# Embedding products on the banks of scores and transposes, two first-stage blocks in the retrievals, six gathered rows in the second stage

## The chip, the cores and the metric

The kernel runs on one core of a Trainium2 chip. The metric is the device time of one execution in microseconds (us), the median of some runs. The engines are called as in the profile: PE (TensorE, matmuls), DVE (VectorE), ACT (ScalarE), POOL (GpSimd, which here only issues gathers), SP (SyncE, which issues the other transfers), and the 16 DMA engines. Every engine works through its own list of instructions in order. A tile framework builds these lists: a planner puts the instructions of the program in an order of its own, by priorities and its own costs, so that the order on an engine need not be the order in the source.

## The reference, cut to what matters

One layer of a decoder for 576 tokens (512 of a prompt, 64 of samples). Attention, a gating unit and their merge come first and are not touched. What matters here is the channel mixer, a retrieval over 16384 experts of one neuron each, and the embedding added after it:

```python
q = (xb @ w_q).reshape(blk, PEER_HEADS, 2, PEER_HALF)
sc = jnp.einsum('thcd,hcnd->thcn', q, sub_keys)
s_top, i_top = lax.top_k(sc, PEER_TOPK)
...
best, pos = lax.top_k(cand, PEER_TOPK)
idx = jnp.take_along_axis(cand_idx, pos, axis=-1)
gate = jax.nn.softmax(best, axis=-1)
act = jax.nn.gelu(jnp.einsum('thkd,td->thk', expert_u[idx], xb))
out = jnp.einsum('thk,thkd->td', gate * act, expert_v[idx])
...
x3 = x2 + sigmoid(rms_norm(x2) @ w_ple_gate) * (p @ w_ple)
```

## The kernel before

The tokens are split in two groups. For 192 of them (the samples and one prompt tile) the chosen rows of `peer_u` and `peer_v` are gathered, one row of 1024 numbers for each of 128 partitions at a time: POOL issues the gather (L726), and DVE multiplies the row and sums it up (L737 for `peer_u`, L744 for `peer_v`). There are 384 such gathered rows (192 of each table).

For the other 384 tokens the mixer is computed densely. A *first-stage block* (`stage1`, L781) multiplies 128 experts of `peer_u` with the 384 tokens: SP loads 512 KB of weights (L75), ACT and DVE split them into a high and a low part (`w_hi` L70, `w_lo` L71), PE runs 24 matmuls of 384 columns (L86), and ACT takes the gelu out of PSUM (L795). There are 128 such blocks. The *second stage* (L977) multiplies the gated result with `peer_v`, 18 matmuls for each of 128 turns (L1022). Blocks of the first stage and turns of the second alternate there until the former have run out.

In between, the gates are needed as a dense matrix. First come five *retrievals* (`retrieve`, L624), a long chain of small DVE instructions that finds for each token the indices and gates of its experts. `make_ew` (L801) transposes the result of one on PE. Then the *gate phase* runs 24 passes (`build_g`, L856; below "pass" 0 to 23), each for 16 tokens in four groups: DVE makes one-hots of the indices (`hot`, L870), ACT or DVE scales them (`og`, L876 or L879), PE multiplies them (eight matmuls, L887), ACT copies the product into the tile `gs` (L891), and at the end of a pass SP writes `gs` to DRAM (`gd`, L894, 1024 KB). `gs` has two buffers, which the passes use in turn. The last two retrievals are still running during the first seven passes.

PE fills its time in the retrievals and in the gate phase with first-stage blocks. Three tables say how many, and how many rows are gathered beside them. `S1_TOPK` is the number of blocks that are to be done by the end of the first, second and third retrieval; each block pays `GP[0]` = 0.5 of a gathered row once gathering has begun. In the gate phase a pass pays `GT[0]` rows for the first seven passes and `GT[1]` for the next fifteen, and the blocks are spread evenly from `S1_TOPK[2]` to 33 (`S1_PRE`) over the first seven passes and to 56 over the others. In the second stage a turn pays `G2[0]` for the first 44 turns, `G2[1]` as long as there are first-stage blocks, and `G2[2]` after that.

During the retrievals PE also computes the embedding products p @ w_ple (`ple`, L819): five tiles of tokens, each in two halves of six matmuls (L837), which ACT copies out (L839). Beside them `x1_rows` (L843) transposes rows of x1 for later (L851).

PSUM has eight banks here: two buffers each of "mm", "sc", "pv" and "pt". First-stage blocks take "mm" and "pv" by turns (L786). The group products of the gate phase take "sc" and "pt" by turns, the transposes of `x1_rows` and `make_ew` take "pt".

Of the kernel before, what the change touches and what calls it, by code (L numbers as in the profile page):

```python
# [25 lines left out]
TB = 16  # L26
JB = 8
GP = [0.5, 0.0, 1.65]
G2 = (1.45, 1.78, 2.06)
SPILL = set(range(2, 40, 2))  # L30
NSP = len(SPILL)
GT = (2.0, 2.9)
GS = 2.0 ** 14
TAIL0 = 112
TAIL1 = 122
S1_TOPK = (4, 9, 13)
TBK = 7
S1_END = 6
OPB = 4
# [12 lines left out]
def tile_decoder_step(ctx: ExitStack, tc: tile.TileContext, a, o):  # L52
# [16 lines left out]
    def split(src, hi, lo):  # L69
        A.activation(hi, src, AF.Copy)  # L70
        V.tensor_sub(lo, src, hi.bitcast(F32))  # L71
# [61 lines left out]
    def bank(tag):  # L133
        return psB.tile([P, 512], F32, name=tag)
# [47 lines left out]
    with tc.high_priority(offset=500):  # L182
        for cols in HALVES:
            ps = bank("sc")[:, :cols.stop - cols.start]
# [64 lines left out]
    for g in range(4):  # L249
# [7 lines left out]
        if g == 0:  # L257
            pv = bank("pt")
# [3 lines left out]
            pv = bank("pt")  # L262
# [279 lines left out]
    for c0, r in tilesA:  # L542
# [4 lines left out]
        for hh in range(2):  # L547
            hs = slice(hh * 512, (hh + 1) * 512)
            pt = bank("pt")
# [182 lines left out]
    def gather_steps():  # L732
        for ti, ns in ((0, NS), (1, P)):
            dots = gp.tile([P, P], F32, name="dots")
            for s in range(ns):
                row_ = gather_row(a["peer_u"], ixs[ti][:, s:s + 1])
                V.scalar_tensor_tensor(row_, row_, 1.0, xrs[ti], op0=ALU.mult, op1=ALU.mult,  # L737
                                       accum_out=dots[:, s:s + 1])
                yield
            A.activation(dots[:, :ns], dots[:, :ns], AF.Gelu_apprx_tanh)  # L740
            V.tensor_tensor(dots[:, :ns], dots[:, :ns], gts[ti][:, :ns], op=ALU.mult)
            for s in range(ns):
                row_ = gather_row(a["peer_v"], ixs[ti][:, s:s + 1])
                V.scalar_tensor_tensor(accs[ti], row_, dots[:, s:s + 1], accs[ti], op0=ALU.mult, op1=ALU.add)  # L744
                yield
# [23 lines left out]
    def pay(x):  # L769
        credit[0] += x  # L770
        n = int(credit[0])
        credit[0] -= n
        gather(n, mark_pe[0])
# [7 lines left out]
    def stage1():  # L781
        nonlocal j1, nlive
        j = j1
        j1 += 1
        w = load_block(a["peer_uT"][j])
        ps = (mm() if j % 2 or phase[0] > 1 else bank("pv"))[:, :NB]  # L786
        tform(ps, w, xb, first=g_last.get(len(g_last) - G_LAG))
        if j in SPILL:
            act = held_x[-1][:, sorted(SPILL).index(j) % 6, :]
        else:  # L790
            n = nlive % RING
            nlive += 1
            act = held_x[n // 6][:, n % 6, :] if n < NXP - 6 else (
                acp[0][:, n - NXP + 6, :] if n < RING - 6 else held_x[-1][:, n - RING + 6, :])
        A.activation(act, ps, AF.Gelu_apprx_tanh)  # L795
        acts[j] = act
        if j in SPILL:
            S.dma_start(ad[sorted(SPILL).index(j)], act)
        pay(GP[phase[0]])

    def make_ew(e0, e1_, gtf):  # L801
        pt = bank("pt")
        for q, src in enumerate((e0, e1_, gtf)):
            T.transpose(out=pt[:, q * P:(q + 1) * P], in_=src, identity=ident)
        ij = ep.tile([P, P // 2, 2, 2], F16, name="ij")
        gpk = ep.tile([P, P, 2], F16, name="gpk")
        for q in range(2):
            A.activation(ij[:, :, q, :], pt[:, q * P:(q + 1) * P].rearrange("p (u t) -> p u t", t=2), AF.Copy)
        V.tensor_scalar(gpk[:, :, 1], pt[:, 2 * P:3 * P], GS, 1.0 / GS, op0=ALU.mult, op1=ALU.max)
        V.scalar_tensor_tensor(gpk[:, :, 0], pt[:, 2 * P:3 * P], GS, gpk[:, :, 1], op0=ALU.mult, op1=ALU.subtract)  # L810
        ewT.append((ij, gpk))
# [7 lines left out]
    def ple():  # L819
        ws_ = []  # L820
        for k in range(2):
            raw = wp.tile([P, D], F32, name="w_raw", bufs=4)
            S.dma_start(raw, a["w_ple"][k])
            ws_.append([plp.tile([P, D], F32R, name=nm) for nm in ("wph", "wpl")])
            split(raw, *ws_[k])
        for c0, r in TILES:
            pt = plp.tile([P, 2, P], F32, name="pt")
            S.dma_start(pt[:, :, :r], a["pT"][:, :, c0:c0 + r])
            ph, pl = (plp.tile([P, 2, P], F32R, name=nm) for nm in ("ph", "pl"))
            split(pt[:, :, :r], ph[:, :, :r], pl[:, :, :r])  # L830
            for hh in range(2):
                st = plp.tile([P, 512], F32, name="st")
                ps = bank("pv")
                hs_ = slice(hh * 512, (hh + 1) * 512)
                for k in range(2):
                    for i, (xi, wi) in enumerate(((ph, 0), (ph, 1), (pl, 0))):
                        T.matmul(ps[:r], lhsT=xi[:, k, :r], rhs=ws_[k][wi][:, hs_],  # L837
                                 start=k == 0 and i == 0, stop=k == 1 and i == 2)
                A.activation(st[:r], ps[:r], AF.Copy)  # L839
                S.dma_start(pld[c0:c0 + r, hs_], st[:r])  # L840
            yield
# [14 lines left out]
    def build_g(tb):  # L856
# [37 lines left out]
        S.dma_start(gd[:, :, tb].rearrange("c p j t -> p c (j t)"), gs.rearrange("p (c j) t -> p c (j t)", j=JB))  # L894

    ples, xrs_ = ple(), x1_rows()
    for ti in range(3):
        for _ in retrieve(ti, ti < 2):
            if len(acts) < S1_TOPK[ti]:
                stage1()  # L900
# [3 lines left out]
        if ti == 0:  # L904
            steps.append(gather_steps())
        while len(acts) < S1_TOPK[ti]:
            stage1()
# [11 lines left out]
    for tb in range(NB // TB):  # L919
# [9 lines left out]
        if tb < TBK:  # L929
            goal = S1_TOPK[2] + (tb + 1) * (S1_PRE - S1_TOPK[2]) // TBK  # L930
        else:
# [6 lines left out]
        for _ in range(2):  # L938
            if rest_t and next(rest_t[0], 1) == 1:
                rest_t.pop(0)  # L940
                make_ew(*found[4 - len(rest_t)])
        pay(GT[tb >= TBK] if tb < 22 else 0)
    while nlive < RING - 1:
# [82 lines left out]
    for j in range(NJ):  # L1026
# [4 lines left out]
        if j and j - 1 not in SPILL and j1 < NJ:  # L1031
            stage1()
        pay(G2[0 if j < 44 else 1 if j1 < NJ else 2])
        if j == TAIL0:
# [185 lines left out]
```

## Time and profile before

| | |
|---|---|
| median of 3 runs | 1717.13 us (1714.81 to 1718.23) |
| the profiled execution | 1715.17 us |
| its span, first to last instruction | 1713.3 us |
| PE, share of the span | 98% |
| DVE | 82% |
| ACT | 47% |
| POOL | 31% |
| DMA, mean rate | 268 GB/s |

The retrievals with the embedding products run from about 497 to 572 us of the span, the gate phase from 575 to 816, with its eighth pass beginning at 661, and the second stage from 837 on. A busy share is a mean over stages with different limits. So the profile is read by stages: which engine is full there, and what each of PE's waits ended on.

### The profile page before, as it was taken

What the parts mean: (1) busy time and instruction counts of PE and PEld (TensorE: products, weight loads), DVE (VectorE), ACT (ScalarE), POOL (GpSimd) and SP (SyncE); (2) the same over time, 40 slices, a digit from 0 to 9 for tenths busy, and PEclk for the clock granted to TensorE, in tenths of its full rate; (3) what the DMA queues carried; (4) which work ended last, traced back from release to release, by engine and by line L of the source; (5) the groups of instructions that cost most, each with busy time, mean ns of one, the idle gap of its engine ahead of it and who ended that gap; (6) DMA issues with size and microseconds to landing.
All of it is one profiled execution on the core that took longest, in us unless ns stands there. A gap on an engine that the chain in (4) does not pass through costs nothing.

```text
span 1713.3 us, 27406 instructions
## 1 busy us (share of the span) xinstructions
PE 1680.2 (98%) x10040; PEld 1518.4 (89%) x10040; DVE 1406.5 (82%) x2725; ACT 806.9 (47%) x1399; POOL 536.2 (31%) x390
## 2 busy tenths in 40 slices
PE   8999999999999999899999999999999999999998
PEld 7988999999988899888988888899999888888877
DVE  7365566569899999898688899989888898999983
ACT  6566452343355888777433333333333433333352
POOL 0000000000002112343144454455565665666600
PEclk9999999999999999999999999999999999999999
DMA  6311222433247789999999999999999899999952
GB/s 235 101 54 59 75 96 87 156 111 103 72 160 262 238 265 303 347 393 359 326 341 367 366 379 396 397 395 369 374 356 365 329 380 344 356 378 375 375 198 80
DMA packets 179479, 459.11 MB, mean 268 GB/s; under 512 B 15504, under 2 KB 78992, under 8 KB 177296
## 3 DMA queue, kind: packets, MB, share of 16 engines
q1 hardware_dynamic: 123760, 255.29, 42.2%
q0 software_dynamic: 55584, 202.07, 31.6%
q8 instruction: 79, 1.29, 0.3%
q14 instruction: 56, 0.46, 0.1%
HBM read 420.67 MB, written 37.36 MB: 267 GB/s over the span
## 4 chain that ended last, share of the span: by engine, by line
PE 86%; DVE 6%; DMA 4%; ACT 3%; issue 1%; SPq 0%; ACTq 0%; DVEq 0%
PE mm L86 40%; PE oacc L1022 31%; PE pv L86 4%; DMA gd<-gs 3%; PE oacc L983 2%; DVE w_lo L71 1%; PE sc L86 1%; PE pt L887 1%; ACT w_hi L70 1%; PE mm L983 1%; PE sc L887 1%; PE sc L596 1%; PE pv L338 1%; ACT og L876 0%; DMA w_raw<-peer_uT 0%
## 5 line engine op out<-in xcount | busy, mean ns | idle before, releaser
L726 POOL DMA_INDIRECT row<-peer_u,idx x192 | 262.8, 1369 | 812.5 <-PE pv L86 470.3
L70 ACT ACTIVATE w_hi<-w_raw 128x1024 fp32r<-128x1024 f32 x321 | 340.0, 1059 | 372.2 <-PE mm L86 279.4
L71 DVE TENSOR_TENSOR w_lo<-w_raw,w_hi 128x1024 fp32r<-128x1024 f32 x321 | 391.4, 1219 | 80.9 <-ACT w_hi L70 79.8
L86 PE MATMUL mm<-xd,w_hi 128*128 128x384 f32 x1552 | 401.6, 337 | 0.0
L726 POOL DMA_INDIRECT row<-peer_v,idx x192 | 272.0, 1417 | 237.8 <-DVE acc L744 159.2
L86 PE MATMUL mm<-x,w_hi 128*128 128x320 f32 (+1 forms) x1504 | 308.1, 299 | 0.0
L86 PEld LDWEIGHTS mm<-xd,w_hi 128*128 128x128 f32 x1552 | 282.0, 188 | 6.5
L86 PE MATMUL mm<-xd,w_lo 128*128 128x384 f32 x776 | 262.0, 338 | 0.0
L744 DVE SCALAR_TENSOR_TENSOR acc<-row,dots,acc 128x1024 f32<-128x1024 f32 x192 | 245.4, 1278 | 4.8 <-DMA row<-peer_v,idx 4.6
L86 PEld LDWEIGHTS mm<-x,w_hi 128*128 128x128 f32 x1504 | 241.8, 190 | 8.2 <-issue 7.4
L737 DVE SCALAR_TENSOR_TENSOR row<-row,xr 128x1024 f32<-128x1024 f32 x192 | 232.1, 1219 | 14.0 <-DMA row<-peer_u,idx 14.0
L1022 PE MATMUL oacc<-w_hi,wh 128*128 128x512 f32 x768 | 241.2, 394 | 0.0
L1022 PE MATMUL oacc<-w_hi,wl 128*128 128x512 f32 x768 | 241.0, 394 | 0.0
L1022 PE MATMUL oacc<-w_lo,wh 128*128 128x512 f32 x768 | 240.9, 394 | 0.0
L86 PE MATMUL mm<-x,w_lo 128*128 128x320 f32 (+1 forms) x752 | 223.1, 297 | 0.0
L1022 PEld LDWEIGHTS oacc<-w_hi,wl 128*128 128x128 f32 x768 | 143.6, 187 | 35.5
L1022 PEld LDWEIGHTS oacc<-w_lo,wh 128*128 128x128 f32 x768 | 143.6, 187 | 35.5
L1022 PEld LDWEIGHTS oacc<-w_hi,wh 128*128 128x128 f32 x768 | 143.0, 187 | 29.4
L86 PEld LDWEIGHTS mm<-xd,w_lo 128*128 128x128 f32 x776 | 146.0, 188 | 0.0
L86 PEld LDWEIGHTS mm<-x,w_lo 128*128 128x128 f32 x752 | 142.4, 189 | 1.0 <-issue 0.8
L86 PE MATMUL pv<-xd,w_hi 128*128 128x384 f32 x496 | 133.8, 345 | 0.0
L70 ACT ACTIVATE wh<-x 128x384 fp32r<-128x384 f32 x66 | 34.6, 525 | 166.0 <-PE oacc L1022 165.9
(331 smaller groups left out, 2119.7 us busy)
## 6 DMA issues: line engine op xcount, KB each, us to landing
w_raw<-peer_uT SPq DMA_DIRECT2D x128, 512.0 KB
w_raw<-peer_v SPq DMA_DIRECT2D x128, 512.0 KB
gd<-gs SPq DMA_DIRECT2D x24, 1024.0 KB
gs<-gd SPq DMA_DIRECT2D x15, 1536.0 KB
w_raw<-w_in SPq DMA_DIRECT2D x30, 512.0 KB
w_raw<-peer_wq SPq DMA_DIRECT2D x16, 512.0 KB
w_raw<-w_br SPq DMA_DIRECT2D x8, 512.0 KB
w_raw<-w_out SPq DMA_DIRECT2D x8, 512.0 KB
```

The lines of the kernel that those rows point to most:

```text
L70: A.activation(hi, src, AF.Copy)
L71: V.tensor_sub(lo, src, hi.bitcast(F32))
L86: mark_pe[0] = T.matmul(ps, lhsT=w[wi][:, wk + k, :], rhs=x[xi][k], start=i == 0, stop=i == n - 1)
L338: ins = T.matmul(pvs[pr, :], lhsT=vt[:, t0 + j, pr], rhs=pT, start=j == 0, stop=j == nj - 1)
L596: T.matmul(ps[:, b * P:(b + 1) * P], lhsT=qp[:, b * P:(b + 1) * P], rhs=sk, start=True, stop=True)
L726: ins = G.indirect_dma_start(out=row_, out_offset=None, in_=table, in_offset=bass.IndirectOffsetOnAxis(ap=ix, axis=0))
L737: V.scalar_tensor_tensor(row_, row_, 1.0, xrs[ti], op0=ALU.mult, op1=ALU.mult, accum_out=dots[:, s:s + 1])
L744: V.scalar_tensor_tensor(accs[ti], row_, dots[:, s:s + 1], accs[ti], op0=ALU.mult, op1=ALU.add)
L887: g_last[tb] = T.matmul(pt[:, t * P:(t + 1) * P], lhsT=hot[:, t // 2, 0, :, t % 2], rhs=right[:, t, :, 1 - h], start=h == 0, stop=h == 1)
L983: T.matmul(p[:r, :hs.stop - hs.start], lhsT=xi[:, k, :r], rhs=w[k][wi][:, hs], start=k == 0 and xi is xh and wi == 0, stop=k == KC - 1 and ...
L1022: mark_pe[0] = T.matmul(oacc[t][hh], lhsT=wi[:, ts], rhs=vi[:, hh * 512:(hh + 1) * 512], start=j == 0 and last == 0 and vi is vh, stop=j = ...
```

## The change

Four numbers and one tag are changed:

```diff
-G2 = (1.45, 1.78, 2.06)
+G2 = (1.45, 1.93, 2.06)
-GT = (2.0, 2.9)
+GT = (2.0, 2.5)
-S1_TOPK = (4, 9, 13)
+S1_TOPK = (4, 10, 15)
...
                 st = plp.tile([P, 512], F32, name="st")
-                ps = bank("pv")
+                ps = bank(("sc", "pt")[hh])
```

The embedding products of a tile use "sc" for the first half and "pt" for the second. Two more blocks of the first stage are due by the end of the third retrieval (15 instead of 13), and two fewer in the first seven passes. The passes from the eighth to the twenty-second pay 2.5 rows instead of 2.9, six fewer in all, and the turns 44 to 85 of the second stage 0.15 rows more each. Worked through with the half rows of the two blocks, 57 rows have been gathered at the end of the gate phase instead of 61, and 308 instead of 307 when the first-stage blocks run out.

On PE, the embedding products of one tile (with the numbers of the buffers; the rows are the end of the first half and the beginning of the second). Before:

```order
L837 MATMUL pv_5987<-wph_5691,ph_5982 128x512
L837 MATMUL pv_5987<-wpl_5692,ph_5982 128x512
L837 MATMUL pv_5987<-wph_5691,pl_5983 128x512
L837 MATMUL pv_5997<-wph_5685,ph_5982 128x512
L837 MATMUL pv_5997<-wpl_5686,ph_5982 128x512
L837 MATMUL pv_5997<-wph_5685,pl_5983 128x512
```

and now:

```order
L837 MATMUL sc_5987<-wph_5691,ph_5982 128x512
L837 MATMUL sc_5987<-wpl_5692,ph_5982 128x512
L837 MATMUL sc_5987<-wph_5691,pl_5983 128x512
L837 MATMUL pt_5997<-wph_5685,ph_5982 128x512
L837 MATMUL pt_5997<-wpl_5686,ph_5982 128x512
L837 MATMUL pt_5997<-wph_5685,pl_5983 128x512
```

The place among the first-stage blocks is the same; only the buffers are others.

On DVE, from the last index of the third retrieval (`e`, L677) to the first one-hot of the gate phase (L870). Before:

```order
L677 TENSOR_TENSOR e_6346<-l_6351 128x128
L645 MAX best<-c_6724 128x8
L686 TENSOR_TENSOR d_6752<-ib 128x8x15
L647 MAX_INDEX pos<-best,c_6724 128x8
L737 SCALAR_TENSOR_TENSOR row,dots<-row,xr 128x1024
L809 TENSOR_SCALAR gpk<-pt 128x128
L870 TENSOR_TENSOR hot<-iota,ij 128x1024
```

Now that piece has 30 rows; these are its last eight, of the fourth and fifth retrieval (L643 to L688) and of a block (L71):

```order
L644 MATCH_REPLACE c_7193<-best,cand 128x50
L643 MAX best<-cand 128x8
L645 MAX best<-c_7193 128x8
L643 MAX best<-cand 128x8 x5
L688 TENSOR_TENSOR ge<-sp,cst 128x2048
L71 TENSOR_TENSOR w_lo<-w_raw,w_hi 128x1024
L809 TENSOR_SCALAR gpk<-pt 128x128
L870 TENSOR_TENSOR hot<-iota,ij 128x1024
```

Up to the first one-hot DVE has 28 instructions of retrievals and two weight splits more than before, and as many gathered rows; the one that stood between index and one-hot is now ahead of the index, with one more. On PE the transposes of `make_ew` (L804), which before stood around the seventeenth block counted from the first retrieval, stand together after the two further blocks.

On DVE, late in the gate phase, between the 58th and the 63rd one-hot. Before:

```order
L737 SCALAR_TENSOR_TENSOR row,dots<-row,xr 128x1024 x2
L71 TENSOR_TENSOR w_lo<-w_raw,w_hi 128x1024
L870 TENSOR_TENSOR hot<-iota,ij 128x1024 x2
L737 SCALAR_TENSOR_TENSOR row,dots<-row,xr 128x1024
L879 TENSOR_TENSOR og<-hot,gpk 128x512
L71 TENSOR_TENSOR w_lo<-w_raw,w_hi 128x1024
L737 SCALAR_TENSOR_TENSOR row,dots<-row,xr 128x1024 x2
L870 TENSOR_TENSOR hot<-iota,ij 128x1024 x3
```

and now:

```order
L71 TENSOR_TENSOR w_lo<-w_raw,w_hi 128x1024
L879 TENSOR_TENSOR og<-hot,gpk 128x512
L870 TENSOR_TENSOR hot<-iota,ij 128x1024 x2
L737 SCALAR_TENSOR_TENSOR row,dots<-row,xr 128x1024
L879 TENSOR_TENSOR og<-hot,gpk 128x512
L737 SCALAR_TENSOR_TENSOR row,dots<-row,xr 128x1024
L870 TENSOR_TENSOR hot<-iota,ij 128x1024
L71 TENSOR_TENSOR w_lo<-w_raw,w_hi 128x1024
L737 SCALAR_TENSOR_TENSOR row,dots<-row,xr 128x1024
L870 TENSOR_TENSOR hot<-iota,ij 128x1024
L737 SCALAR_TENSOR_TENSOR row,dots<-row,xr 128x1024
L870 TENSOR_TENSOR hot<-iota,ij 128x1024
```

Five rows have become four, and they alternate with one-hots. Over the whole piece from the first one-hot of pass 7 to the first one of pass 23 there are 37 rows instead of 45 and 21 weight splits instead of 23. On PE the last pass ends in the fifty-sixth block instead of at the end of the fifty-seventh, counted from the first retrieval, so that over six blocks stand between it and the second stage instead of five.

## The prediction

> **What bounds the kernel now.** I read the page's first lines first, then the list of who waited for whom on PE. Its columns are: total us, times, longest.
>
> ```profile
> PE 1680.2 (98%) x10040; PEld 1518.4 (89%) x10040; DVE 1406.5 (82%) x2725; ACT 806.9 (47%) x1399; POOL 536.2 (31%) x390
> PE pt L887 <- ACT og L876: 7.3, 4, 4.7
> PE mm L202 <- ACT x L175: 6.7, 1, 6.7
> PE pv L837 <- ACT x L795: 6.6, 3, 3.4
> PE sc L887 <- ACT og L876: 4.2, 4, 1.7
> PE pt L804 <- DVE e L677: 0.7, 1, 0.7
> ```
>
> PE is busy for 98% of the span, and the change neither adds nor removes a matmul. So the time can only move by what PE waits, and by its clock. The 6.7 us at L202 are the start of the kernel and stay. What is left are 6.6 us in the embedding products (L837) and 11.5 us in the gate products (L887). The busy times of five stretches show where that is (retrievals, gate phase before and after its seventh pass, hand-over, and two of the second stage):
>
> ```profile
> core 0: us, PE busy (x) PEld busy (x) DVE busy (x) ACT busy (x) POOL busy (x), PEclk, DMA share, GB/s
> 497.00:572.00 75.00, 67.39 (x356) 61.41 (x355) 70.92 (x294) 45.55 (x62) 11.87 (x9) 0.95 0.73 244
> 572.00:661.00 89.00, 88.56 (x641) 82.70 (x639) 88.07 (x211) 78.37 (x165) 16.26 (x12) 1.00 0.82 260
> 661.00:808.00 147.00, 137.29 (x1084) 126.46 (x1083) 133.15 (x204) 114.92 (x280) 59.88 (x45) 0.98 1.04 365
> 808.00:837.00 29.00, 27.06 (x167) 26.35 (x165) 11.61 (x18) 14.89 (x31) 0.00 (x0) 0.94 0.85 299
> 1050.00:1100.00 50.00, 50.00 (x244) 43.93 (x243) 47.68 (x79) 17.99 (x24) 24.67 (x18) 1.00 1.01 398
> 1122.00:1474.00 352.00, 352.00 (x1766) 317.00 (x1765) 311.96 (x413) 126.06 (x170) 207.06 (x145) 1.00 0.97 362
> ```
>
> PE is idle for 7.6, 0.4, 9.7 and 1.9 us in the first four, 19.6 in all, and for nothing in the second stage. The column PEclk adds a second loss: PE runs at half clock for a while after some of the waits.
>
> ```profile
> 524.00:538.00 14.00, 10.64 (x45) 9.38 (x44) 11.89 (x23) 9.00 (x13) 1.88 (x1) 0.76 0.97 359
> 697.00:706.00 9.00, 4.95 (x28) 4.25 (x28) 4.72 (x7) 5.50 (x14) 1.80 (x2) 0.62 1.05 353
> 808.00:816.00 8.00, 6.06 (x45) 5.35 (x43) 0.81 (x2) 5.42 (x16) 0.00 (x0) 0.79 0.69 225
> ```
>
> 14 us at 0.76, 9 at 0.62 and 8 at 0.79 are 3.4 + 3.4 + 1.7 = 8.5 us of clock. I estimate that 2 of these lie inside the waits. So 26 us are to be had at most, about 9.5 before the gate phase and 16 in it.
>
> **Part 1, the embedding products leave "pv".** The timeline of PE and ACT at the longest of the three waits:
>
> ```profile
> 524.03 0.39 PE L837 MATMUL pv<-wph,ph 128*128 128x512 f32 x1
> 528.91 0.79 PE L837 MATMUL pv<-wph,ph 128*128 128x512 f32 x1 [3.36 <-ACT x L795]
> 525.75 1.28 ACT L795 ACT_TABLE_LOAD   x1
> 527.04 0.49 ACT L795 ACTIVATE x<-mm 128x384 f32<-128x384 f32 x1
> 528.37 0.48 ACT L795 ACTIVATE x<-pv 128x384 f32<-128x384 f32 x1
> ```
>
> "pv" has two buffers, and every other first-stage block fills one. The second half of an embedding tile must wait until ACT has taken the last block out (528.37), and ACT is late by two table loads. On "sc" and "pt", which nothing but the row copies uses then, this wait goes: 6.6 us, and the 2.7 of half clock that I count outside it. The ACT and SP work of these tiles is the same as before.
>
> What is late next is DVE. It is busy for 70.92 of 75 us in the retrievals and for 88.07 of 89 after them, and the gate phase cannot begin before DVE has made the third tile's indices and one-hots. So I count DVE's own idle time from 497 to 661:
>
> ```profile
> DVE w_lo L71 <- ACT w_hi L70: 1.2, 2, 1.0
> DVE ge L705 <- ACT sp L651: 1.0, 1, 1.0
> DVE den L700 <- ACT gate L698: 0.8, 1, 0.8
> DVE row L737 <- DMA row<-peer_u,idx: 0.7, 1, 0.7
> DVE ge L688 <- ACT sp L651: 0.6, 1, 0.6
> ```
>
> The first three are ACT instructions that stood behind a copy or a weight buffer held up by PE; they go, 3.0 us. The other two stay.
>
> **Part 2, two blocks into the retrievals.** A block is 24 matmuls and takes 4.18 us, from one start to the next line's:
>
> ```profile
> 1206.21 0.52 PE L86 MATMUL mm<-xd,w_hi 128*128 128x384 f32 x2
> 1210.39 0.63 PE L1022 MATMUL oacc<-w_hi,wh 128*128 128x512 f32 x2
> L71 DVE TENSOR_TENSOR w_lo<-w_raw,w_hi 128x1024 fp32r<-128x1024 f32 x321 | 391.4, 1219 | 80.9 <-ACT w_hi L70 79.8
> L737 DVE SCALAR_TENSOR_TENSOR row<-row,xr 128x1024 f32<-128x1024 f32 x192 | 232.1, 1219 | 14.0 <-DMA row<-peer_u,idx 14.0
> ```
>
> Two blocks are 8.4 us of PE, 2.4 of DVE (L71), and two 512 KB loads on SP's queue: moved, not added. They also pay half a credit each, so one more gathered row (1.2 us of DVE) comes before the gate phase. On PE the change reaches the transposes of L804 with 8.4 us more work and 6.6 + 0.3 + 0.7 + 2.7 = 10.3 us less waiting, at 571.8 + 8.4 - 10.3 = 569.9; DVE's last index comes at 571.7 - 3.0 + 1.2 = 569.9, at the same time.
>
> ```profile
> 571.75 0.33 PE L804 MATMUL pt<-c_ident,e 128*128 128x128 f32 x1 [0.66 <-DVE e L677]
> 573.38 0.68 DVE L870 TENSOR_TENSOR hot<-iota,ij 128x1024 f16<-128x1024 f16 x1
> 575.52 0.70 PE L887 MATMUL sc<-og,hot 128*128 128x128 f16 x8
> ```
>
> But the new order on DVE puts 28 small instructions (70.92 us for 294 is 0.24 each, so up to 6.7; I take 5.2, as most of them are shorter than that mean) and two weight splits (2.4) ahead of the first one-hot, and one row (1.2) less. It starts 2.0 - 1.2 + 7.6 = 8.4 us behind the index, at 578.3, and the first gate product 2.1 later, at 580.4. PE has 1.46 blocks (6.1 us) before it and arrives at 576: a new wait of some 4 us takes the old one's place. It is not lost twice, since DVE has that work done earlier. At the first one-hot of the eighth pass DVE has done the same splits, one-hots and retrieval work in both orders, and one row more: -3.0 + 1.2 = **-1.8 us**, my value for parts 1 and 2. Bounds: -10.3 if DVE does not bind; +2 if none of its idle time goes and half a clock loss comes on top.
>
> The Trainium skill ("TensorE: Matmul & The Clock Gate", Part 1) says that the clock halves after an idle window of about 3.4 us; the waits of 3.36 and 4.7 us agree, but three shorter ones (1.7, 0.5, 1.9 us from 802 to 810) were followed by 0.79 too. By that rule the new wait of 4 us costs up to 3.4 us more, and the sum would be 1713; by the rows PE has the slack to run slowly then, and I add nothing.
>
> **Part 3, fewer rows in the gate phase.** ACT's wait behind the 11.5 us is this one (ACT's waits, 661 to 837; then issue on SP and end on ACT of two cases, and the queues of 661 to 808):
>
> ```profile
> ACT gs L891 <- DMA gd<-gs: 13.5, 5, 5.2
> 685.61 0.38 SPq L894 DMA_DIRECT2D gd<-gs  x1
> 698.78 0.60 ACT L891 ACTIVATE gs<-sc 128x512 f32<-128x512 f32 x1 [5.21 <-DMA gd<-gs]
> 660.05 0.43 SPq L894 DMA_DIRECT2D gd<-gs  x1
> 668.71 0.60 ACT L891 ACTIVATE gs<-sc 128x512 f32<-128x512 f32 x1 [0.50 <-DMA gd<-gs]
> q1 hardware_dynamic: 36899, 29.84, 61.6%
> q0 software_dynamic: 6486, 23.60, 42.2%
> ```
>
> "gs" has two buffers, so pass k waits for the write of pass k-2: 13.2 us late in the phase against 8.7 early, with the DMA share at 1.04 against 0.82. The DMA engines set the pace. The queue of the gathered rows took 42.2% of 147 us for 45 rows: 1.38 us a row. From the first one-hot of pass 7 to that of pass 23 DVE's order has 37 rows instead of 45 and 21 weight splits instead of 23. At 1.38 us each (a weight load has a row's size) that is 13.8 us of DMA, 13.3 at a share of 1.04. The two blocks come back as 8.4 us of PE after the last pass, where nothing is waited for. Net **-4.9 us**. Bounds: -15 if all waits and half clocks of the phase go; +5 by the third rival.
>
> **Part 4, rows in the second stage.** 42 turns of 0.15 are 6.3 rows: 7.7 us of DVE and 8.7 of DMA in 352. PE does not wait there at a DMA share of 0.97, nor from 1050 to 1100 at 1.01, and DVE is free for 40 us of 352. I cost it at nothing; were DMA the bound, it would be 8.7.
>
> The profiled execution took 1715.2 us (span 1713.3), 2.0 below the median of the runs shown (1717.1). 1715.2 - 1.8 - 4.9 = 1708.5, and 1710.5 as a median: **1710**.
>
> **Rivals.** *Both waits really go.* DVE has 14 us of idle time from 661 to 808 to make good a late start, and the rows that leave are the ones that crowd the write. With two thirds of the 9.5 us and of the 16 us: -17, 1700. Against it: DVE is full from 572 to 661. Chance 0.22.
> *The waits are exchanged.* PE waits at L804 and L887 for DVE what it waited at L837, the phase with "gs" gains 1 to 3 us, and the change does not do what its parts say: 1715. For it: DVE's 98%. Chance 0.20.
> *Slower.* With fewer blocks between the gate products the passes lie closer: counted through PE's order at its pitch, from the last product of pass k to the first of pass k+2 it is 9.1 us on average instead of 10.9. If the write still lands 11 us after its issue (the mean of the two cases quoted), the waits that I count through from pass to pass add up to 17 us instead of 13.5, and two more of over 3 us bring half clock, 3.4 each: +10.3 - 1.8, 1725. It decides at a landing of about 11 us. Chance 0.10.
> My forecast, 1705 to 1713.5, has 0.48.
>
> **How the numbers follow.** A measurement of this kernel can tell about 0.2% (3.4 us). Faster by more: 0.46 of my 0.48 and 0.22 = 0.68; within: 0.20 + 0.02 = 0.22; slower: 0.10. The range reaches to most of the first rival and all of the second, and leaves out 2 in 10 (the third rival and the far ends of the others): 1700 to 1719.
>
> **What would show it.** No wait of L837 on L795; a wait of about 4 us before the first gate product; under 2 us of DVE idle from 497 to the eighth pass; L891 waiting less than 13.5 us for the write; a PE without idle time in the second stage, and more blocks after the last pass. It is wrong if the eighth pass starts over 5 us earlier (DVE did not bind), or if the write's waits grow.

## The result, and the profile after

| | before | after |
|---|---|---|
| median, 5 runs each on one chip | 1715.69 us (1714.40 to 1718.23) | 1724.23 us (1723.95 to 1727.06) |
| ratio after / before | | 1.0052, 95% interval 1.0037 to 1.0067 |
| span of the profiled execution | 1713.3 us | 1722.1 us |
| first product of pass 7 | 661.1 | 658.5 |
| from there to the last gate product (L887) | 154.9 | 158.9 |
| from there to the first L1022 | 21.3 | 27.2 |
| from there to the end of the span | 876.0 | 877.6 |

The change made the kernel 0.5% slower, by 8.5 us. The last four rows add up to the span; the starts are those of the L887 and L1022 groups in the timeline. Pass 7 begins 2.7 us earlier, the late gate phase is 4.0 us longer instead of 13.3 shorter, 5.9 us of blocks come behind it, and the second stage costs 1.6. A few executions took 2027 to 8112 us; no ratio counts them, the medians of e1 and e3 below each count one, which moves them by 0.2 us, and the profile of e10 was taken from one and is not read.

The page's first line of the kernel after:

```profile
PE 1680.4 (98%) x10040; PEld 1519.7 (88%) x10040; DVE 1405.3 (82%) x2725; ACT 805.7 (47%) x1399; POOL 545.6 (32%) x390
```

PE is busy for the same 1680 us as before. Its waits (total us, times, longest):

```profile
PE pt L887 <- ACT og L876: 15.3, 8, 4.5
PE pt L851 <- DMA xc<-x1d: 7.3, 1, 7.3
PE mm L202 <- ACT x L175: 6.7, 1, 6.7
PE sc L887 <- ACT og L876: 3.9, 2, 3.5
PE oacc L1022 <- DVE w_lo L71: 1.2, 1, 1.2
```

L837 waits no more, but L851, a row-copy transpose in the same stage, waits 7.3 us for a load. The gate products (L887) wait 19.2 us where they waited 11.5. The stretches that answer to those of before (retrievals, early and late gate phase, hand-over, a piece of the second stage):

```profile
core 0: us, PE busy (x) PEld busy (x) DVE busy (x) ACT busy (x) POOL busy (x), PEclk, DMA share, GB/s
497.00:581.00 84.00, 76.51 (x420) 72.05 (x420) 81.45 (x334) 53.20 (x75) 13.50 (x10) 0.96 0.74 243
581.00:658.50 77.50, 76.66 (x573) 71.44 (x572) 77.19 (x167) 69.22 (x153) 16.78 (x12) 1.00 0.86 277
658.50:811.00 152.50, 133.57 (x1038) 121.79 (x1038) 123.94 (x190) 114.13 (x280) 50.81 (x39) 0.94 0.95 320
811.00:844.50 33.50, 33.50 (x212) 32.90 (x210) 16.58 (x25) 15.97 (x31) 1.85 (x2) 1.00 0.92 314
844.50:1196.50 352.00, 352.00 (x1706) 308.70 (x1705) 313.10 (x413) 125.83 (x170) 178.88 (x128) 1.00 0.98 373
```

The loss is in the third row: 18.9 us without PE (9.7 before), a clock of 0.94 (0.98), while the DMA share fell from 1.04 to 0.95 and the rate from 365 to 320 GB/s. The rows that left did take their transfers with them; the stage is longer all the same. DVE, at 124 of 152 us, has room too. The half-clock stretches in it:

```profile
689.00:695.00 6.00, 5.29 (x28) 4.86 (x28) 4.63 (x7) 4.68 (x13) 2.22 (x2) 0.72 0.93 306
706.00:715.00 9.00, 5.03 (x28) 4.63 (x28) 4.34 (x8) 3.79 (x8) 2.43 (x3) 0.62 1.02 392
768.00:777.00 9.00, 6.62 (x34) 5.98 (x34) 5.47 (x8) 5.18 (x11) 1.15 (x1) 0.62 0.83 270
```

1.7 + 3.4 + 3.4 = 8.5 us of clock, where before had one stretch of 3.4 there and one of 1.7 in its last pass (808 to 816), 5.1 in all.

The 158.9 us also hold less work than the 154.9 of before: 22.6 blocks instead of 24.2 by their matmuls (L86) in the trace, 6.5 us less. Up to the first L1022 both kernels do the same, the products of passes 7 to 23 and some 29 blocks, and there it is 186.1 us against 176.1. PE is idle for 18.9 of them instead of 11.6, and 3.4 us more of clock are lost. These two are 10.7 us, the whole 10.0 within what such counts are good for.

What PE waits for is read on ACT, first its wait for the write of `gs` (658 to 811):

```profile
ACT gs L891 <- DMA gd<-gs: 22.3, 8, 6.3
```

Then the third of the stretches in the timeline (start, length, engine and line; in brackets the idle time before and its releaser):

```profile
754.87 0.38 SPq L894 DMA_DIRECT2D gd<-gs  x1
762.19 0.45 SPq L894 DMA_DIRECT2D gd<-gs  x1
768.20 0.60 ACT L891 ACTIVATE gs<-sc 128x512 f32<-128x512 f32 x1 [6.34 <-DMA gd<-gs]
769.14 0.37 PE L887 MATMUL pt<-og,hot 128*128 128x128 f16 x2 [4.20 <-ACT og L876]
770.75 0.95 PE L887 MATMUL pt<-og,hot 128*128 128x128 f16 x6 [1.24 <-ACT og L876]
```

Pass 16's write is issued at 754.87 and pass 18's first copy, into the same buffer, can start at 768.20, 13.3 us later. ACT stands for 6.3 us; behind it on ACT stand the scalings of `og` (L876) for the next group, and PE stands for them. The wait on ACT grew from 13.5 us before to 22.3.

### The profile page after: what moved, and what is told of

The parts are those of the page before. It is cut to its first block, busy times and chain, and to the rows that moved or that the text cites. A ratio compares the mean times of both kernels' runs of the same rounds, so it can differ in the third digit from the quotient of the medians.

```text
span 1722.1 us, 27420 instructions
## 1 busy us (share of the span) xinstructions
PE 1680.4 (98%) x10040; PEld 1519.7 (88%) x10040; DVE 1405.3 (82%) x2725; ACT 805.7 (47%) x1399; POOL 545.6 (32%) x390
## 4 chain that ended last, share of the span: by engine, by line
PE 67%; issue 9%; POOL 9%; DMA 7%; DVE 4%; ACT 3%; SPq 0%; POOLq 0%; ACTq 0%; DVEq 0%
PE mm L86 31%; PE oacc L1022 20%; POOL row L726 9%; PE pv L86 5%; DMA gd<-gs 4%; PE oacc L983 2%; PE sc L86 1%; DVE w_lo L71 1%; DMA row<-peer_v,idx 1%; PE sc L596 1%; ACT w_hi L70 1%; PE mm L983 1%; PE pt L887 1%; ACT og L876 1%; PE sc L887 1%
## 5 line engine op out<-in xcount | busy, mean ns | idle before, releaser
L71 DVE TENSOR_TENSOR w_lo<-w_raw,w_hi 128x1024 fp32r<-128x1024 f32 x321 | 391.2, 1219 | 76.9 <-ACT w_hi L70 76.0
L86 PE MATMUL mm<-xd,w_hi 128*128 128x384 f32 x1552 | 401.9, 338 | 0.0
L726 POOL DMA_INDIRECT row<-peer_v,idx x192 | 281.4, 1466 | 175.9 <-DVE acc L744 152.3
L86 PE MATMUL mm<-x,w_hi 128*128 128x320 f32 (+1 forms) x1504 | 308.1, 299 | 0.0
L86 PEld LDWEIGHTS mm<-xd,w_hi 128*128 128x128 f32 x1552 | 282.7, 189 | 6.3
L86 PE MATMUL mm<-xd,w_lo 128*128 128x384 f32 x776 | 262.7, 339 | 0.0
L86 PEld LDWEIGHTS mm<-x,w_hi 128*128 128x128 f32 x1504 | 241.8, 190 | 8.2 <-issue 7.4
L737 DVE SCALAR_TENSOR_TENSOR row<-row,xr 128x1024 f32<-128x1024 f32 x192 | 232.3, 1218 | 16.7 <-DMA row<-peer_u,idx 16.7
L1022 PE MATMUL oacc<-w_lo,wh 128*128 128x512 f32 x768 | 241.0, 394 | 1.2 <-DVE w_lo L71 1.2
L1022 PE MATMUL oacc<-w_hi,wl 128*128 128x512 f32 x768 | 241.1, 394 | 0.0
L1022 PE MATMUL oacc<-w_hi,wh 128*128 128x512 f32 x768 | 241.1, 394 | 0.0
L86 PE MATMUL mm<-x,w_lo 128*128 128x320 f32 (+1 forms) x752 | 223.1, 297 | 0.0
L1022 PEld LDWEIGHTS oacc<-w_lo,wh 128*128 128x128 f32 x768 | 143.5, 187 | 37.0 <-DVE w_lo L71 1.6
L1022 PEld LDWEIGHTS oacc<-w_hi,wl 128*128 128x128 f32 x768 | 143.6, 187 | 35.6
L1022 PEld LDWEIGHTS oacc<-w_hi,wh 128*128 128x128 f32 x768 | 143.0, 187 | 29.3
L86 PEld LDWEIGHTS mm<-xd,w_lo 128*128 128x128 f32 x776 | 146.6, 189 | 0.0
L86 PEld LDWEIGHTS mm<-x,w_lo 128*128 128x128 f32 x752 | 142.3, 189 | 1.0 <-issue 0.8
L86 PE MATMUL pv<-xd,w_hi 128*128 128x384 f32 x496 | 133.8, 344 | 0.0
```

The source lines that it names most:

```text
L86: mark_pe[0] = T.matmul(ps, lhsT=w[wi][:, wk + k, :], rhs=x[xi][k], start=i == 0, stop=i == n - 1)
L726: ins = G.indirect_dma_start(out=row_, out_offset=None, in_=table, in_offset=bass.IndirectOffsetOnAxis(ap=ix, axis=0))
L1022: mark_pe[0] = T.matmul(oacc[t][hh], lhsT=wi[:, ts], rhs=vi[:, hh * 512:(hh + 1) * 512], start=j == 0 and last == 0 and vi is vh, stop=j = ...
```

## The experiments

Each was timed against the kernel before on the same chip; a ratio is to that kernel.

**One part at a time.** The edits, from the kernel before:

```diff
# e1, banks
-                ps = bank("pv")
+                ps = bank(("sc", "pt")[hh])
# e2, blocks
-S1_TOPK = (4, 9, 13)
+S1_TOPK = (4, 10, 15)
# e3, rows
-G2 = (1.45, 1.78, 2.06)
+G2 = (1.45, 1.93, 2.06)
-GT = (2.0, 2.9)
+GT = (2.0, 2.5)
```

e4 has the first two of these edits, e6 (further down) the last two.

> The kernel before with the embedding products on the banks sc and pt alone. Both theories agree on the early part: the three waits of L837 on L795 (6.6 us) go and DVE's idle time falls by up to 3.0 us, with no block and no row moved; the first product of pass 7 comes 2 to 4 us earlier than 661.1. Late part (first product of pass 7 to the first L1022, 176.1 us before): unchanged within 2 us, since the order of passes, rows and blocks there is that of before. Theory 'reuse' (the write of gs lands some 11 us after its issue whatever the rate; passes that lie closer wait longer): 1711 to 1714. Rival 'bank' (the move to sc and pt itself brings the new PE wait of 7 us at L851 and its half clock, and that is the loss): a wait of L851 on the load of xc here too, and 1720 or more.

> The kernel before with two blocks moved into the retrievals alone. Early: the waits of L837 may stay (the bank pv is still shared), and one row more stands ahead of the gate phase: the first product of pass 7 from 2 us earlier to 2 us later than 661.1. Late: counted through PE's order, the mean distance from the last product of pass k to the first of pass k+2 is that of before (8.2 us by this count in both, for passes 7 to 21). Theory 'reuse': waits of L891 for the write no larger than before (13.5 us), late part 173 to 177, time 1711 to 1716. Rival 'fewer blocks between the passes from this move' (the two blocks that left are what the late passes lack): waits of L891 over 18 us and 1720 or more.

> The kernel before with the rows alone moved from the gate phase to the second stage (GT and G2). The clean test. Counted through PE's order the distance from pass k to k+2 falls from 8.2 to 7.4 us. Theory 'reuse' (a landing some 11 us after the issue, whatever the row count): the waits of L891 for the write grow from 13.5 to over 20 us, PE's waits in the gate products from 11.5 to 17 or more; the pass from tile 7 to the end of tile 23 gets shorter by less than the PE work that left it, and the time is 1719 to 1727. Theory 'rate' (the DMA engines' rate sets the pace, as the prediction had it): 13 us of DMA leave, the waits shrink below 13.5, and the time is 1706 to 1712.

> The kernel after without its move of rows (bank and blocks alone). Theory 'reuse': the early part comes as in the kernel after (first product of pass 7 at 657 to 660, with or without a wait on xc at L851, since DVE binds), the late waits of L891 are no larger than before, so the time is 1709 to 1714, faster than before by 0.1 to 0.4%. Rival 'early' (the wait on xc and its half clock are what the change loses): 1720 or more here too. Rival 'blocks' (the two moved blocks are what the late passes lack): 1720 or more, with late waits over 18 us.

| kernel | median | ratio, 95% interval |
|---|---|---|
| e1 banks | 1717.22 | 0.9998 (0.9979 to 1.0016) |
| e2 blocks | 1718.07 | 1.0003 (0.9986 to 1.0020) |
| e3 rows | 1722.69 | 1.0026 (1.0009 to 1.0042) |
| e4 banks and blocks | 1717.63 | 0.9995 (0.9977 to 1.0012) |

Banks and blocks bring no gain or loss that is clear of the noise, together or alone. The interval of e4 holds my -1.8 us (0.9990) as well as nothing, but not the loss of the whole change. Its 1709 to 1714 us and those of e1 and e2 did not come, and the write's waits in e1, e2 and e4 were 18.0, 17.4 and 17.9 us, where I expected no more than before's 13.5 in e2 and e4. The rows alone lose, about half of what the whole change loses. The distance of "8.2 and 7.4 us" in the expectations of e2 and e3 is, by how I counted it, that from one pass to the next, not from k to k+2 as the words say; the count of the later runs is the right one. In e1, PE's and DVE's waits (DVE from 497 us to pass 7):

```profile
PE pt L851 <- ACT st L839: 8.0, 1, 8.0
DVE ge L705 <- ACT sp L651: 1.3, 1, 1.3
DVE row L737 <- DMA row<-peer_u,idx: 0.8, 1, 0.8
DVE ge L688 <- ACT sp L651: 0.6, 1, 0.6
```

No wait of L837 is left, a wait of 8.0 us at L851 stands in its place, and the first one-hot of the gate phase comes at 570.9 us, where it also comes in e3 (571.0) without that wait. e3 runs the same instructions as before up to its tenth pass, with the old waits of L837:

```profile
PE pv L837 <- ACT x L795: 6.0, 3, 2.3
DVE ge L705 <- ACT sp L651: 1.2, 1, 1.2
DVE row L737 <- DMA row<-peer_u,idx: 0.8, 1, 0.8
DVE ge L688 <- ACT sp L651: 0.6, 1, 0.6
ACT gs L891 <- DMA gd<-gs: 20.7, 10, 6.0
```

DVE idles for 2.6 us here, and pass 7 begins at 658.7, as early as in the kernel after. So the DVE idle time that I put down to L837 isn't tied to it. The last row (ACT, 658 to 811) is the finding: with eight rows fewer up to the last pass, the write is waited for 20.7 us.

**How far one execution stands from another**, and the pair of edits still missing, blocks with rows:

> The kernel before once more, profiled in another execution, to see how far one execution's stages stand from another's. The kernel with the rows alone runs the same instructions as this one up to the tenth pass, and its pass 7 began at 658.7 us, not at 661.1. If that was the execution and not the edit, pass 7 begins here anywhere from 658 to 662, DVE's idle time from 497 us to pass 7 is anywhere from 2 to 4.5 us, and the waits of L891 for the write are 13 to 19 us. If the stages repeat within 0.5 us, pass 7 begins at 661 again and the waits are 13 to 14 us.

> The kernel after without the move to the banks sc and pt (blocks and rows alone). Its order of passes on PE is that of the kernel after. If the banks play no part in the loss: 1720 to 1727, waits of L891 for the write over 20 us, three waits of L837 on L795 as before. Rival 'bank' (the move of banks adds to the loss through L851): 1717 to 1720, like rows alone or less.

```profile
DVE ge L705 <- ACT sp L651: 1.6, 1, 1.6
DVE w_lo L71 <- ACT w_hi L70: 1.0, 1, 1.0
DVE row L737 <- DMA row<-peer_u,idx: 0.8, 1, 0.8
DVE ge L688 <- ACT sp L651: 0.6, 1, 0.6
ACT gs L891 <- DMA gd<-gs: 16.7, 5, 8.4
```

The second execution of before (DVE to 660, ACT from 658): pass 7 begins at 660.0, DVE idles 4.0 us, the write is waited for 16.7 us, and pass 7 to the last gate product takes 157.4 us instead of 154.9. Stages of one profile are good to 2 or 3 us, so the 2.7 that pass 7 gained means little, and the write's wait grew from 13.5, 16.7 or 18.0 us (the last in e1, which has the order of before there) to 22.3. e6 took 1729.21 us, 1.0063 (1.0040 to 1.0087), a little above the expected 1727, with a wait of 22.1: the loss is there without the banks.

**The same order with a faster write.** `gd` is laid out so that a pass is written in runs of 8 KB; the second stage then reads runs of 512 B. Bytes and order of instructions on every engine are unchanged.

```diff
-    gd = dr.tile([NJ // JB, P, NB // TB, JB, TB], F32, name="gd")
+    gd = dr.tile([P, NB // TB, NJ, TB], F32, name="gd")
-        S.dma_start(gd[:, :, tb].rearrange("c p j t -> p c (j t)"), gs.rearrange("p (c j) t -> p c (j t)", j=JB))
+        S.dma_start(gd[:, tb], gs)
-                S.dma_start(gsl[:, :nb], gd[j // JB][:, :nb])
+                S.dma_start(gsl[:, :nb], gd[:, :nb, j:j + JB])
```

> The kernel after, with gd laid out so that a pass is written in runs of 8 KB per partition instead of 16 runs of 512 B; the second stage then reads it in runs of 512 B. The same bytes, and the same order of instructions on every engine. Theory 'reuse' (the passes wait for a landing, and the landing is long because the write's short packets stand between the packets of rows and weights): the landing falls from about 10 us to 5 to 7, the waits of L891 for the write from 22.3 to under 10 us, the stretch from pass 7 to the last gate product from 158.9 to 146 to 151, and the time to 1710 to 1716, if the second stage hides the short reads (PE does not wait there). Theory 'rate' (the bytes that the engines must move set the pace): the bytes are the same, the waits stay over 18 us, and the time 1720 to 1726. If the second stage is bound by DMA, the short reads there cost up to 10 us, and the gain of the gate phase is given back.

> The kernel before with that layout of gd. Theory 'reuse': the waits of L891 fall from 13.5 to 18 us to under 6, the stretch from pass 7 to the last gate product from 155 to 158 to 144 to 150, and the time to 1705 to 1712, faster than before by 0.3 to 0.6%. With the waits gone in both, the kernels before and after should lie within 0.2% of each other. Theory 'rate': as before, within 0.2%.

In e7, ACT's wait (658 to 811) and the largest of PE's:

```profile
ACT gs L891 <- DMA gd<-gs: 9.7, 6, 5.0
PE mm L86 <- DVE w_lo L71: 25.4, 7, 7.1
```

And its late gate phase and the first part of its second stage:

```profile
659.00:796.00 137.00, 129.45 (x1045) 118.45 (x1044) 125.49 (x193) 114.40 (x282) 55.23 (x40) 0.99 0.95 360
829.00:1181.00 352.00, 326.59 (x1516) 285.19 (x1515) 281.08 (x366) 112.02 (x151) 159.44 (x112) 0.96 0.94 333
```

From pass 7 to the last gate product it takes 142.4 us instead of 158.9, with the wait down to 9.7; in e8 142.6 instead of 154.9 to 157.4, with 3.2. So in both kernels this phase shortens with the write's wait, at the same bytes. The two are not yet equal: e7 has 1.5 blocks fewer in that stretch, and up to the first L1022 it takes 169.5 us against 163.9 in e8. The 7.5 to 10.0 us by which the kernel after is behind there have become 5.6, with 6.5 us more of wait left in e7 than in e8, and the medians are 0.24% apart instead of 0.5%. The whole is slower (1741.97, 1.0134, 1.0109 to 1.0158; e8 1737.77, 1.0120, 1.0095 to 1.0146), because the short reads cost the second stage 37 us (914.3 to the end of the span in e7, 877.6 in the kernel after), far over the 10 that I allowed: in its first 352 us PE waits 25.4 us for late weights. The times that I expected of e7 and e8 were missed for that reason. The test leaves one thing open: 2048 packets of 512 B took 28 ns each and 128 of 8 KB 319 ns, on 16 engines 3.6 us a write against 2.6, so the new layout also frees engine time. The next runs keep the bytes and the layout.

**The room between the passes.** Counted through PE's order at its pitch (from one matmul's start to the next, 0.174 us in a block, 0.058 in a gate product) for passes 7 to 21: how far a pass's first and last group lie apart, and the room from the last group of pass k to the first of pass k+2, in which k's write has to land. `S1_END` shifts where the planner puts the blocks.

```diff
# e9, from the kernel after; e11, from before (e10, from after, has 4)
-S1_END = 6
+S1_END = 8
# e12, from before
-        S.dma_start(gd[:, :, tb].rearrange("c p j t -> p c (j t)"), gs.rearrange("p (c j) t -> p c (j t)", j=JB))
+        A.dma_start(gd[:, :, tb].rearrange("c p j t -> p c (j t)"), gs.rearrange("p (c j) t -> p c (j t)", j=JB))
```

> The kernel after with two blocks more left behind the last pass (S1_END 8), the rows as in the kernel after. Counted through PE's order at its pitch, for passes 7 to 21: the four groups of a pass lie within 4.7 us instead of 6.1, and from the last group of pass k to the first of pass k+2 there are 10.1 us instead of 8.7 (before: 5.3 and 10.6). Theory 'room' (a pass waits when PE's order leaves less between the last group of k and the first of k+2 than the write takes to land, some 10 us): the waits of L891 for the write fall from 22 to 8 to 15 us, the stretch from pass 7 to the last gate product from 159 to 143 to 150, the two blocks come back as 8.4 us behind it, and the time is 1713 to 1719. Rival 'rate' (the DMA work of the phase sets its length): the bytes are the same, the waits stay at 18 to 25, and the two blocks behind the last pass bring 1722 to 1733.

> The kernel after the other way: two blocks fewer behind the last pass (S1_END 4). In PE's order the four groups of a pass lie within 5.8 us and the room from k to k+2 is 7.9 us, less than in the kernel after (8.7). Theory 'room': the waits of L891 grow to 24 to 32 us and the time is 1723 to 1731. Rival 'rate': the same bytes, waits of 18 to 25, and two blocks fewer behind the last pass, 1714 to 1722.

> The kernel before with S1_END 8 alone. A pass lies within 4.5 us instead of 5.3 in PE's order, the room from k to k+2 is 10.6 us in both. Theory 'room': the waits of L891 stay about as before, 12 to 20 us, the stretch is shorter by the blocks that left it (up to 5 us) and these come back behind it: 1712 to 1719, within 0.3% of before. Rival 'rate': the stretch keeps its length (157), and the blocks come on top: 1721 to 1726.

> The kernel before with the write of gs issued on ACT's queue, so that it no longer stands behind weight loads on SP's. The order of passes changes with it (a pass within 5.0 us, room 10.2). If the landing of some 10.6 us is mostly the wait of its first packet behind the loads issued ahead of it (2 to 5 us in most late passes), the landing falls to 7 or 8, the waits of L891 to under 8 and the time to 1705 to 1713. If it is the sharing of the engines with rows and weights whatever the queue, the landing stays at 10 or more, and the time at 1715 to 1722.

e9: 1711.89 us, 0.9966 (0.9951 to 0.9981), faster than both kernels, with the rows where the change puts them. ACT's wait in it (655 to 850):

```profile
ACT gs L891 <- DMA gd<-gs: 12.6, 6, 5.0
```

Its late gate phase and hand-over:

```profile
658.00:798.00 140.00, 131.45 (x1046) 120.69 (x1045) 125.74 (x194) 116.16 (x282) 56.93 (x40) 0.96 1.02 356
798.00:832.00 34.00, 32.77 (x202) 31.87 (x202) 16.12 (x23) 15.91 (x30) 0.00 (x0) 1.00 0.93 321
```

The same rows and writes as in the kernel after now pass in 146.4 us instead of 158.9, at a DMA share of 1.02 instead of 0.95. The 8.4 us that I expected back behind the last pass didn't come (27.7 against 27.2): 22.5 blocks lie in the stretch, 22.6 in the kernel after. What changed is how evenly they lie. e10 went the other way, 1726.88 us, 1.0059 (1.0042 to 1.0076), as the room has it and against the rival's 1714 to 1722. e11: 1715.91, 0.9986 (0.9968 to 1.0004), with a wait of 10.7, a time as the room has it. But its stretch stays at 154.8 us although 5 us of blocks left it, as the rival had expected: more of its waits were followed by half clock, which took 8.4 us (5.1 in before). e12: 1745.99, 1.0163 (1.0136 to 1.0190), neither of the two outcomes: the wait for the write fell to 6.5 us and the mean landing to 8.2, but the queue changed the planner's order, and DVE now waits for ACT's halves of the weights:

```profile
DVE w_lo L71 <- ACT w_hi L70: 40.0, 20, 5.7
```

With the DMA share down to 0.87 from 673 to 850 us, the shorter landing can come from the queue or from the slower phase, so e12 does not settle the queue's worth.

**What stayed open: the new wait at L851, and the blocks.**

```diff
# e13, from the kernel after
-                xc = plp.tile([P, 4, P], F32, name="xc")
+                xc = plp.tile([P, 4, P], F32, name="xc", bufs=3)
# e16, from the kernel after
-GT = (2.0, 2.5)
+GT = (2.0, 2.7)
-S1_END = 6
+S1_END = 8
```

e14 is e3 with `S1_END` 8, e15 is e4 with `S1_END` 7.

> The kernel after with a third buffer for xc, so that the last load of xc is issued earlier on SP; the order on PE, DVE and ACT is that of the kernel after. Theory 'DVE binds the early part': the wait of L851 for xc (7.3 us on PE) and the half clock behind it go, and turn up as a wait of PE for DVE ahead of the first gate product; the first gate product stays at 579.5 to 582, pass 7 at 657.5 to 661, time within 0.2% of the kernel after (1721 to 1728). Rival 'PE': pass 7 begins 5 to 9 us earlier and the time is 1714 to 1718.

> Rows alone (no bank, no blocks) with S1_END 8. A pass within 5.0 us in PE's order, room from k to k+2 9.75 us (rows alone: 5.9 and 8.5). Theory 'room': waits of L891 for the write from 20.7 down to 10 to 16 us, 1710 to 1717, like the kernel after with S1_END 8 (1711.9). If the moved blocks cost by themselves, this is faster than that one by 3 us or more (1709 or less); if they help, it is slower by 3 or more.

> Banks and blocks without the move of rows, with S1_END 7. A pass within 4.6 us, room 11.0 us, the largest of all orders tried; the rows stay in the gate phase. If room is all: waits of L891 of 6 to 13 us and 1708 to 1713. If the rows' DMA also counts (each row lengthens the landing of the writes beside it): landing over 11 us, waits of 12 to 18 and 1713 to 1718, slower than the kernel after with S1_END 8.

> The kernel after with S1_END 8 and half of the rows put back into the gate phase (GT 2.7). A pass within 4.6 us, room 10.6 us. If room is all: waits of 7 to 13 us and 1709 to 1713, no slower than with GT 2.5 (room 10.1). If the rows' DMA counts as much as the room, 1711 to 1716.

e13: 1725.30, 1.0053 (1.0034 to 1.0072), no gain; but the wait didn't go, it changed its releaser:

```profile
PE pt L851 <- ACT st L853: 6.6, 1, 6.6
```

The load was earlier, and PE stood for a copy instead; the first gate product stays at 580.9. That agrees with DVE as the bound, but the case of a PE that doesn't wait there was not reached. In e13 the write is waited for 23.3 us. e14: 1717.78, 1.0008 (0.9993 to 1.0024). e15: 1714.22, 0.9982 (0.9969 to 0.9995). e16: 1712.83, 0.9977 (0.9962 to 0.9991). e14 is 0.8 us over the range of "room"; e15 came out as the theory has it in which the rows' DMA counts too, and so did e16 by its wait, while its time fits both. All orders of one layout side by side; "lands" is the mean from the issue (L894) to the last packet for passes 7 to 21, counted off the trace's packets in their order, good to about half a us; "late" is from pass 7 to the last gate product, "to L1022" from pass 7 to the first L1022:

| kernel | pass | room | lands | room - lands | wait on ACT | late | to L1022 | ratio |
|---|---|---|---|---|---|---|---|---|
| before, twice | 5.3 | 10.6 | 10.6, 10.4 | 0, 0.2 | 13.5, 16.7 | 154.9, 157.4 | 176.1, 178.6 | 1 |
| e4 banks, blocks | 5.0 | 10.9 | 11.4 | -0.5 | 17.9 | 158.2 | 179.3 | 0.9995 |
| e3 rows | 5.9 | 8.5 | 9.7 | -1.2 | 20.7 | 149.8 | 181.3 | 1.0026 |
| after | 6.1 | 8.7 | 9.8 | -1.1 | 22.3 | 158.9 | 186.1 | 1.0052 |
| e9 after, END 8 | 4.7 | 10.1 | 10.1 | 0 | 12.6 | 146.4 | 174.1 | 0.9966 |
| e11 before, END 8 | 4.5 | 10.6 | 10.9 | -0.3 | 10.7 | 154.8 | 181.3 | 0.9986 |
| e14 rows, END 8 | 5.0 | 9.8 | 10.0 | -0.2 | 12.2 | 145.8 | 175.6 | 1.0008 |
| e15 banks, blocks, END 7 | 4.6 | 11.0 | 11.1 | -0.1 | 17.2 | 159.9 | 182.2 | 0.9982 |
| e16 after, GT 2.7, END 8 | 4.6 | 10.6 | 11.0 | -0.4 | 14.0 | 150.9 | 176.7 | 0.9977 |

Where the room falls over 1 us short of the landing, ACT waits 21 to 22 us (22.1 and 23.3 in e6 and e13, with the passes of after); where they are about equal, 11 to 18 (18.0 in e1, with those of before). Rows beside a write do lengthen its landing (10.4 to 11.4 us with all of them, 9.7 to 10.1 without the eight), so both terms count.

"late" holds 21.7 blocks in e3 and 24.2 in before, "to L1022" 29.1 to 29.3 in every kernel, so the latter compares like with like. There the mean room is not all: e11 and e15 come out close to e3, with a smaller shortfall. What the kernels differ by is what PE loses, its idle time plus the lost clock (summed over windows of 4 us): 17 and 19 us in before, 27 in after, 15 in e9 and e14, 21 in e11, 22 in e3, 24 in e15. Without it every one has 158 to 162 us. Waits that are followed by half clock cost more than others of the same length, which a mean room doesn't show.

What stays open: e14 and e9 have the same wait, the same late phase and spans of 1713.0 and 1712.1, yet the medians are 0.4% apart, by which the blocks help there. The profiles can't show why, since the profiled execution of e14 lay 3.0 us under its median and that of e9 2.1 above. And the blocks cost 0.3% beside the rows without `S1_END` 8 (e6 and after against e3), where room and landing are alike. Whether blocks and banks help or hurt beside the moved rows is not settled by these runs. A third `gs` buffer, 8 KB more of each partition, which would give each write another pass to land in, was not tried.

## Why the prediction was wrong

- **Parts 1 and 2.** The first one-hot was forecast at 578.3 and came at 578.6, the first gate product at 580.4 and came at 580.6; L837's wait went. The new PE wait came, but 7.3 us long and at L851, ahead of the transposes of L804 (574.2), not behind them. -1.8 us was of the size of the 2.7 seen, but e3 and e5 show that pass 7 moves by that much with the same code, and e4 puts both parts at 0.9995, with an interval that holds nothing and -1.8 alike: the runs do not confirm the figure. The reason given for the 3.0 of DVE idle (ACT instructions held up by PE) falls: e3 idles 2.6 with PE's waits in place. The frame, that DVE binds up to the eighth pass, held as far as it was tested: PE's wait there changed its line, its length and its releaser (e1, after, e13) without moving the time.
- **Part 3 is the step that failed:** "The DMA engines set the pace." I took the rows' 13.3 us of DMA off the stage as time. Rows did leave (share 1.04 to 0.95; up to the last product 40 gathers instead of 45), but the stage went from 154.9 to 158.9. What sets its length is the turn of two `gs` buffers: a pass is written, the write lands, the pass after next may begin. Fewer rows shortened the landing by some 0.7 us, but the new tables moved the blocks so that the room fell by 1.9 and a pass got 0.8 longer; the edit of the rows alone does that (e3). e9 shows it from the other side: with the blocks spread evenly, the same rows and the same bytes give 146.4. Against e15, which has all rows, e9's late phase is 13.5 us shorter and the time behind it 5.4 longer (27.7 against 22.3), which looks like the forecast's -13.3 and +8.4. It is no support for them: 5.4 us of that are blocks moved behind the last pass, e15's profiled execution was the slowest of its twelve, and between the medians 2.3 us are left. The mechanism accounts for the rows' share of the loss (0.26% in e3); why the blocks add as much again beside the moved rows stays open.
- **The blocks behind the last pass** were put at 8.4 us; 5.9 came, since 6.5 blocks stand there instead of 5.1.
- **Part 4** was put at nothing, 8.7 if DMA bound: 1.0 to 1.6 us (876.0 and 876.6 to 877.6), of which 1.2 is PE's wait at L1022. Right in the main, but the cover is thin: the 512-B reads of e7 cost 37 us there.
- **The rival "Slower"** named this mechanism and its point ("It decides at a landing of about 11 us") and gave 1725, within 1 us of the median. It expected 17 us of waits and two more half-clock stretches; 22.3 us and two stretches came. That the time fits so well is partly luck: the room was 8.7 us by the later count, not 9.1, the mean landing 9.8, not 11, and the second stage cost 1.6. Its chance of 0.10 was too low. What spoke for it, the shorter distance, could be counted in PE's order, while "the DMA engines set the pace" rested on two writes and a share of 1.04, which a stage that waits for landings shows as well.

- **What would show it:** the list's own last sign, "if the write's waits grow", is what came; DVE's idle time (2.1 us by its waits, against "under 2") and the second stage's were near what it named.

## What to carry to other kernels

A double buffer that is written out costs its whole turn: fill, land, refill. Before moving work out from between its uses, count the room that is left in the order of the engine that fills it and set it against the landing seen in the trace; a full DMA share doesn't say that fewer bytes make the turn shorter. And take a second profile of the unchanged kernel before a gap of 2 or 3 us is explained.

## What the runs showed that was not expected

The same 1 MB write took some 5 us from issue to last packet where no gather was issued in between (5.0 and 5.4 in passes 22 and 23 of the second execution of before), and 13 to 17 with six row gathers issued in between, beside weight loads (pass 8: 13.3 in that execution, 16.8 in e4). The Trainium skill ("DMA: Bandwidth & Descriptors", "Queues, rings and completion order") says that each DMA engine goes round its queues packet by packet. No run here shows an engine's turn. In keeping with it, 512-B packets of 28 ns stand beside row packets of 4 KB and 171 to 181 ns, and 8-KB runs cut the mean landing from 9.8 to 7.6 us in the same order; but these runs also take less engine time, as said above.
